# First experts of a two-block kernel: two fixed places instead of four, the plan four steps earlier, four places of 32 slots

## The chip, the cores and the metric

The kernel runs on one core of a Trainium2 chip, in one launch. The metric is the device time of that launch in microseconds (us). The kernel before took 2408.33 us as the median of three runs (2404.2 to 2413.0). One more execution was profiled; every row below comes from that one.

## What is computed

512 tokens of 1024 numbers go through two transformer blocks. Each block has a mixer (attention and a second branch) and a mixture of experts. The change concerns the experts of the first block alone:

```python
def hierarchical_moe(u, w_grp, b_grp, w_exp, b_exp, w_e_gate, w_e_up, w_e_down):
    ...                                    # every token picks 2 of 16 experts, with weights
    for e in range(N_EXPERTS):             # 16
        h = jax.nn.silu(t @ w_e_gate[e]) * (t @ w_e_up[e])     # 1024 -> 512
        y = y + comb[:, e:e + 1] * (h @ w_e_down[e])           # 512 -> 1024
```

Everything is float32. The three weights of an expert are 2 MB each, so the 16 experts read 96 MB. The 1024 assignments fall unevenly. Worked out from the reference's inputs, experts 0 to 15 get 27, 49, 13, 41, 17, 17, 29, 17, 96, 103, 87, 72, 131, 77, 77 and 171 tokens.

## The kernel before

**Stages.** First mixer, first experts (`moe1`), second mixer, second experts (`moe2`), one after the other on all engines. `moe1` and `moe2` share the function `experts`; its argument `nh` is 1 for `moe1` and 2 for `moe2`, and picks the tables at the top of the file.

**Places.** `experts` works through 16 places, in a fixed order. A place is a number of token slots and the weights of one expert. The first `FIXED` places hold experts 0, 1, ... by number, so that they can start before anybody knows how many tokens each expert has. The other places get the remaining experts by rank of their token count: `plan` (L839) computes the ranks on chip, and a table of constants says which rank goes to which place. Before, places 0 to 3 are fixed, with 128 slots each; places 6 and 11 are pairs (128 and 64 slots, `PAIRS`); of the rest, 5, 7, 9 and 12 have 96 slots, 8, 10, 13 and 15 have 64 (`SLOTS`), and 4 and 14 have 128. If an expert has more tokens than its place has slots, a loop at the end of `experts` makes one more pass for the rest.

**Work of a place.** `prep` builds a list of the place's tokens as a table of ones and zeros (`list_hot`, `oh`; on VectorE for the fixed places, on GpSimd for the others), TensorE multiplies it out (`prep2`, `pt<-paux,oh`), VectorE turns it into row numbers (`list_end`), GpSimd gathers the rows (`x_gather`, `xg`), and TensorE turns them (`x_turn`). Then come the products with gate and up (`gu`, into PSUM tiles `pm`), the activation, a turn of its result (`act_turn`), the product with down (`dn`, into `po`), and a scatter that adds the rows to `Y` in memory (`y_scatter`).

**Two kinds of product.** In places of 96 slots and more, each weight tile is split into a high part `whi` (ScalarE, L118) and a low part `wlo` (VectorE, L119), and each product is three matmuls, of 512 columns each: 48 for `gu` and 24 for `dn`. A pair adds 48 more for its second 64 slots. In places of 64 slots (`col`), the weight tile `wraw` is used as it is, in a slower float32 form that the trace records as two matmuls for each product, and gate and up stand side by side in two halves of the array (`col_gu`, `col_dn`): 32 records for `gu` and 16 for `dn`.

**Weights.** Gate and up of a place are two loads of 1 MB each, down is two more, so a place has six. The order of loads is that of use: `gu` of a place (4 loads), then `dn` of the place before it (2). They go to a ring of seven buffers. Four loads are issued before the stage, three by GpSimd at its start, and each further one by SyncE when the buffer seven loads back is free. A buffer is free when both its halves are split; in `col` places only when the matmuls have read it, for gate and up only when both have been read.

**Order.** The loop at the end of `experts` writes the instructions of each engine step by step, a step for each load; `at(step, f)` hangs other work on a step. `plan` is a generator whose parts hang on steps 0 to 6; the list of a place hangs `LEAD` steps (15, 12, 11, 10) ahead of its first product, its turns 5 and 2 steps ahead. `ctx_steps` hangs preparations of the second mixer on steps 6 to 88; `ctx_load` loads two last pieces for it.

## Time and profile before

| | us |
|---|---|
| median of three runs | 2408.33 |
| the profiled execution | 2409.98 |
| its span on the core | 2408.2 |
| in it, the last row of the router to the first product of an expert | 372 to 387 |
| products of the first experts | 387 to 716 |
| from there to the first load of the second mixer's rows | 716 to 727 |

The 1.8 us between the profiled execution's time and its span lie around the span. TensorE is busy 89% of the span, VectorE 57%, ScalarE 43%, GpSimd 28%. A busy TensorE is a matmul in flight; since matmuls overlap, the time from one start to the next tells its pace, not the length of one. In the first experts' stage the granted clock of TensorE is mostly the full 2.4 GHz.

### The profile page before, as it was taken

What the parts mean: (1) busy time and instruction counts of PE and PEld (TensorE: products, weight loads), DVE (VectorE), ACT (ScalarE), POOL (GpSimd) and SP (SyncE); (2) the same over time, 40 slices, a digit from 0 to 9 for tenths busy, and PEclk for the clock granted to TensorE, in tenths of its full rate; (3) what the DMA queues carried; (4) which work ended last, traced back from release to release, by engine and by line L of the source; (5) the groups of instructions that cost most, each with busy time, mean ns of one, the idle gap of its engine ahead of it and who ended that gap; (6) DMA issues with size and microseconds to landing.
All of it is one profiled execution on the core that took longest, in us unless ns stands there. A gap on an engine that the chain in (4) does not pass through costs nothing. (4 is left out here: it accounts for less than half of the span.)

```text
span 2408.2 us, 31803 instructions
## 1 busy us (share of the span) xinstructions
PE 2150.7 (89%) x11269; PEld 1395.7 (58%) x11269; DVE 1383.2 (57%) x2666; ACT 1037.6 (43%) x1577; POOL 681.6 (28%) x610
## 2 busy tenths in 40 slices
PE   6999986998988999999969899979999789988982
PEld 2655655775646886778857555635656445545520
DVE  5555697985647956653387555545555265527412
ACT  3333445874544444542236444324444244425301
POOL 2001235524323020000035343424344244333301
PEclk9999897999998999999979999989999989999996
DMA  8767447998977333323458999899999899999996
GB/s 275 246 204 263 170 158 263 376 338 304 360 270 215 86 96 122 90 65 115 140 193 302 345 401 393 305 378 401 397 393 368 301 403 377 386 395 401 382 415 231
DMA packets 208869, 681.65 MB, mean 283 GB/s; under 512 B 21261, under 2 KB 61029, under 8 KB 161601
## 3 DMA queue, kind: packets, MB, share of 16 engines
q1 hardware_dynamic: 185280, 607.88, 67.3%
q0 software_dynamic: 23136, 70.64, 10.7%
q8 instruction: 91, 1.49, 0.2%
q10 hardware_dynamic: 288, 1.05, 0.1%
q14 instruction: 74, 0.60, 0.1%
HBM read 642.69 MB, written 36.90 MB: 282 GB/s over the span
## 5 line engine op out<-in xcount | busy, mean ns | idle before, releaser
L119 DVE TENSOR_TENSOR wlo<-wraw,whi 128x1024 fp32r<-128x1024 f32 (+1 forms) x559 | 676.5, 1238 | 318.8 <-ACT whi L118 310.8
L118 ACT ACTIVATE whi<-wraw 128x1024 fp32r<-128x1024 f32 (+1 forms) x559 | 572.3, 1053 | 319.1 <-PE pm L81 120.8
L81 PE MATMUL pm<-whi,xh 128*128 128x512 f32 (+1 forms) x736 | 304.4, 414 | 3.5 <-ACT whi L118 3.5
L81 PE MATMUL pm<-wlo,xh 128*128 128x512 f32 (+1 forms) x736 | 297.5, 407 | 1.3 <-DVE wlo L119 1.2
L1196 POOL DMA_INDIRECT Y<-eo,isc x52 | 102.4, 1969 | 593.2 <-ACT eo L1195 251.5
L81 PE MATMUL pm<-whi,xl 128*128 128x512 f32 (+1 forms) x640 | 260.8, 407 | 0.0
L81 PE MATMUL pm<-wraw,xh 128*64 128x512 f32 (+1 forms) x1280 | 245.1, 614 | 14.9 <-DMA wraw<-in_w_gu 14.9
L81 PEld LDWEIGHTS pm<-whi,xh 128*128 128x128 f32 (+1 forms) x736 | 136.4, 185 | 47.3 <-ACT whi L118 4.2
L927 POOL TENSOR_SCALAR oh<-slots,plan 128x64 bf16<-128x64 f32 (+3 forms) x168 | 157.4, 1045 | 0.3
L81 PEld LDWEIGHTS pm<-wlo,xh 128*128 128x128 f32 (+1 forms) x736 | 130.3, 177 | 42.7 <-DVE wlo L119 2.6
L993 POOL DMA_INDIRECT xg<-U,ig x52 | 93.2, 1792 | 199.1 <-issue 112.6
L81 PEld LDWEIGHTS pm<-wraw,xh 128*64 128x64 f32 (+1 forms) x1280 | 65.8, 128 | 141.0 <-issue 108.3
L81 PEld LDWEIGHTS pm<-whi,xl 128*128 128x128 f32 (+1 forms) x640 | 116.7, 182 | 38.6 <-issue 0.9
L81 PE MATMUL po<-wraw,ah 128*64 128x512 f32 (+1 forms) x640 | 126.1, 606 | 14.0 <-DMA wraw<-in_w_dn 13.6
L81 PE MATMUL po<-whi,ah 128*128 128x512 f32 (+1 forms) x320 | 128.3, 401 | 0.0
L81 PE MATMUL po<-whi,al 128*128 128x512 f32 (+1 forms) x320 | 125.8, 393 | 0.9 <-DVE al L1160 0.9
L81 PE MATMUL po<-wlo,ah 128*128 128x512 f32 (+1 forms) x320 | 125.7, 393 | 0.0
L1005 PEld LDWEIGHTS pt<-ident,xg 64*128 64x128 f32 (+3 forms) x416 | 57.3, 197 | 80.2 <-DMA xg<-U,ig 34.4
L1005 PE MATMUL pt<-ident,xg 64*128 64x64 f32 (+3 forms) x416 | 69.6, 291 | 38.2 <-DMA xg<-U,ig 36.6
L1016 DVE TENSOR_TENSOR xl<-pt,xh 128x512 fp32r<-128x512 f32 (+1 forms) x52 | 32.5, 625 | 122.2 <-ACT xh L1014 122.0
L1014 ACT ACTIVATE xh<-pt 128x512 fp32r<-128x512 f32 (+2 forms) x60 | 31.3, 522 | 147.0 <-PE pt L1005 138.0
L81 PEld LDWEIGHTS po<-wraw,ah 128*64 128x64 f32 (+1 forms) x640 | 35.7, 127 | 90.9 <-issue 60.7
(618 smaller groups left out, 3994.8 us busy)
## 6 DMA issues: line engine op xcount, KB each, us to landing
wraw<-in_w_gu SPq DMA_DIRECT2D x254, 1024.0 KB
wraw<-in_w_dn SPq DMA_DIRECT2D x127, 1024.0 KB
wraw<-in_w_e_down SPq DMA_DIRECT2D x32, 1024.0 KB
wraw<-in_w_e_up SPq DMA_DIRECT2D x31, 1024.0 KB
wraw<-in_w_e_gate SPq DMA_DIRECT2D x30, 1024.0 KB
wraw<-in_w_in SPq DMA_DIRECT2D x58, 512.0 KB
mz<-in_w_ada SPq DMA_DIRECT2D x80, 256.0 KB
wraw<-in_w_mod SPq DMA_DIRECT2D x26, 512.0 KB
```

The costliest lines, as they stand in the source:

```text
L81: self.nc.tensor.matmul(out, lhsT, rhs, start=start, stop=stop)
L118: nc.scalar.activation(h, v, AF.Copy)
L119: nc.vector.tensor_sub(l, v, h.bitcast(F32))
L927: (eng or self.nc.gpsimd).tensor_scalar(oh[:, c, :], self.slots[:, 0:n], poscol(c), None, op0=OP.is_equal)
L993: self.nc.gpsimd.indirect_dma_start(out=B.xg[0:B.n, :], out_offset=None, in_=self.U, in_offset=bass.IndirectOffsetOnAxis(ap=B.ig[:, :1], a ...
L1005: self.nc.tensor.transpose(B.xt[:, k * n:k * n + n], B.xg[0:n, 4 * h2 + k:1024:8], self.ident[0:n, 0:n])
L1014: nc.scalar.activation(B.xh[:, d, 0:n], pv, AF.Copy)
L1016: nc.vector.tensor_sub(lo, pv, B.xh[:, d, 0:n].bitcast(F32))
L1196: nc.gpsimd.indirect_dma_start(out=self.Y[:, :], out_offset=bass.IndirectOffsetOnAxis(ap=B.isc[:, :1], axis=0), in_=o, in_offset=None, com ...
```

## The change

Six tables change, all for `nh` = 1. Two places are fixed instead of four. The pairs are places 4 and 10. Places 6, 8, 12, 14 and 15 have 96 slots, 5 and 9 have 64, 2, 3, 7 and 11 have 32; 0, 1 and 13 have 128. In all there are 1504 slots, before 1792. With the token counts above, each of the experts has a place that holds it, before and after; the tightest is the fourth of the movable ones, 96 tokens in 96 slots. The six parts of `plan` hang on steps -4, -3, -1, 0, 1 and 2, and lists of places that need the plan not before step 3.

In a place of 32 slots `col_gu` has four products side by side: gate and up of two slices of the inner dimension at a time, whose halves `col_act` (new) adds up. `dn` of `col` places is now done by `row_dn`, which also takes four at a time there, and the scatter adds the halves.

```diff
-FIXED = {2: 2, 1: 4}
-PAIRS = {2: (7, 16), 1: (6, 11)}
+FIXED = {2: 2, 1: 2}
+PAIRS = {2: (7, 16), 1: (4, 10)}
...
+PLAN = {2: (0, 1, 2, 3, 4, 5), 1: (-4, -3, -1, 0, 1, 2)}
...
-         1: ((5, 7, 9, 12), (8, 10, 13, 15))}
+         1: ((6, 8, 12, 14, 15), (5, 9), (2, 3, 7, 11))}
...
+        for a in range(2):
             for s, v in enumerate((gv, uv)):
-                self.mm(B.pg[hf, s], B.xf[:, j, 0:64], v[:, k, :], j == 0, j == 7)
+                k = 2 * q + a
+                p = n * (s + 2 * a if B.col == 4 else s)
+                j = 4 * kk + k
+                self.mm(B.pg[p:p + n], B.xf[:, j, 0:n], v[:, k, :], j == (a if B.col == 4 else 0),
+                        j == (6 + a if B.col == 4 else 7))
+
+    def col_act(self, B, stage):
+        nc, ea, n = self.nc, self.ea, B.n
+        if stage == 0:
+            a = B.a = ea.tile([128, 512], F32, name="ea")
+            if B.col == 4:
+                b = B.b = ea.tile([128, 512], F32, name="eb")[0:64]
+                nc.scalar.activation(b, B.pg[0:64], AF.Copy)
+                nc.vector.tensor_add(b, b, B.pg[64:128])
+                nc.scalar.activation(a[32:64], b[0:32], AF.Silu)
+            else:
+                nc.scalar.activation(a[0:64], B.pg[0:64], AF.Silu)
+        elif B.col == 4:
+            nc.vector.tensor_mul(B.b[0:32], B.b[32:64], B.a[32:64])
+            B.b = B.b[0:32]
...
-        for i in range(7):
+        for i in PLAN[nh]:
             at(i, next, plan, None)
...
+                for i, f in enumerate(((prep, b, B), (prep2, B), (prep3, B), (self.x_gather, B))):
+                    at(max(s0 - lead[i] - o, PLAN[nh][-1] + 1 + i if b >= fixed else -99), *f)
                 for h2 in range(2):
-                    at(s0 - lead[4 + h2] - o, self.x_turn, B, h2)
-                    at(s0 - lead[4 + h2] - o + 0.5, self.x_split, B, h2)
+                    i = max(s0 - lead[4 + h2] - o, PLAN[nh][-1] + 5 + h2 if b >= fixed else -99)
+                    at(i, self.x_turn, B, h2)
+                    at(i + 0.5, self.x_split, B, h2)
...
-                                self.col_dn(B, hf, s, raws[i], q, hf == nh - 1)
+                            elif what == "dn" and q == 0:
+                                self.row_dn(B, 0, s, raws[i], True)
```

Where this moves instructions most is the start of the stage. On GpSimd, before, the plan stands around the gather of place 2, and the first list that needs it (128 slots, `oh<-slots,plan`) comes after the gather of place 3:

```order
L853 TENSOR_SCALAR plank<-slots 128x4
L854 TENSOR_TENSOR plano<-plank,ident 16x16
L993 DMA xg<-U_111,ig 128x1024
L857 TENSOR_SCALAR plano<-plank,planc 16x16
...
L882 TENSOR_SCALAR bpos<-plan 128x4 x2
L1499 DMA rows_3832<-in_ctx 128x1024
L993 DMA xg<-U_111,ig 128x1024
L270 DMA gsc<-mod_108 128x8
L927 TENSOR_SCALAR oh<-slots,plan 128x128 x4
```

On GpSimd at the same point after the change:

```order
L855 TENSOR_SCALAR plank<-slots 128x2
L856 TENSOR_TENSOR plano<-plank,ident 16x16
L859 TENSOR_SCALAR plano<-plank,planc 16x16
...
L884 TENSOR_SCALAR bpos<-plan 128x4 x2
L929 TENSOR_SCALAR oh<-slots,plan 128x32 x8
L929 TENSOR_SCALAR oh<-slots,bpos 128x64 x4
L1515 DMA rows_3836<-in_ctx 128x1024
L995 DMA xg<-U_111,ig 32x1024 x2
```

The gathers of places 2 and 3 now stand behind the whole plan and behind twelve list operations, eight of them for these two places.

On TensorE before, where place 0 starts (`pt<-ident,xg` are turns of gathered rows, `pm<-whi,xh` is the first product):

```order
L1005 MATMUL pt<-ident,xg 128x128 x8
...
L1005 MATMUL pt<-ident,xg 128x128 x4
L81 MATMUL pm<-whi,xh 128x512
L81 MATMUL pm<-wlo,xh 128x512
```

On TensorE at the same point after the change:

```order
L1007 MATMUL pt<-ident,xg 128x128 x8
L867 MATMUL pt<-ident,pos 16x128 x4
L1007 MATMUL pt<-ident,xg 128x128 x4
L83 MATMUL pt<-planm,plant 128x16 x5
L83 MATMUL pm<-whi,xh 128x512
L83 MATMUL pm<-wlo,xh 128x512
```

The plan's first nine matmuls stood among the products of place 0 and now stand ahead of the first of them.

## Rows read from the trace of the kernel before

**Rows 1.** Windows: start:end, length, busy by engine (count), clock, DMA share, GB/s

```profile
372.00:387.00 15.00, 4.47 (x25) 3.40 (x25) 8.25 (x42) 2.90 (x5) 5.81 (x10) 0.50 0.63 221
387.00:520.00 133.00, 128.44 (x606) 100.74 (x607) 116.97 (x182) 104.71 (x132) 71.96 (x72) 0.97 1.01 371
520.00:600.00 80.00, 71.69 (x341) 46.47 (x341) 48.19 (x85) 43.27 (x68) 30.79 (x25) 0.99 0.86 289
600.00:716.00 116.00, 113.66 (x516) 68.84 (x516) 65.19 (x83) 59.33 (x80) 30.99 (x23) 0.99 0.90 329
716.00:727.00 11.00, 0.00 (x0) 0.00 (x0) 0.76 (x2) 0.68 (x1) 1.40 (x1) 0.60 0.42 67
```

**Rows 2.** Timeline of SyncE: start, length, issue of a load

```profile
655.50 0.34 SPq L105 DMA_DIRECT2D wraw<-in_w_e_gate  x1
668.95 0.33 SPq L105 DMA_DIRECT2D wraw<-in_w_e_up  x1
```

**Rows 3.** Timeline of TensorE: split products, then a place of 64 slots

```profile
655.24 0.39 PE L81 MATMUL po<-wlo,ah 128*128 128x512 f32 x1
...
664.09 0.39 PE L81 MATMUL pm<-whi,ah 128*128 128x512 f32 x1
...
665.27 3.65 PE L81 MATMUL pm<-wraw,xh 128*64 128x512 f32 x16
...
669.50 3.65 PE L81 MATMUL pm<-wraw,xh 128*64 128x512 f32 x16
```

**Rows 4.** DMA queues from 387 to 706: packets, MB, share of 16 engines

```profile
DMA packets 18152, 109.74 MB, mean 344 GB/s; under 512 B 2387, under 2 KB 2899, under 8 KB 6739
...
q1 hardware_dynamic: 13215, 92.95, 75.3%
q0 software_dynamic: 4917, 16.53, 19.7%
```

**Rows 5.** Groups by shape in 1200 to 2000, TensorE (second experts): busy, mean ns

```profile
L81 PE MATMUL pm<-wraw,xh 128*32 128x512 f32 x320 | 42.2, 643 | 0.0
...
L81 PE MATMUL po<-wraw,ah 128*32 128x512 f32 x160 | 23.1, 596 | 3.4 <-DMA wraw<-in_w_dn 3.3
```

**Rows 6.** Groups in 387 to 716, VectorE and ScalarE: busy, mean ns, idle before

```profile
L119 DVE TENSOR_TENSOR wlo<-wraw,whi 128x1024 fp32r<-128x1024 f32 x144 | 173.0, 1226 | 35.8 <-ACT whi L118 34.2
...
L118 ACT ACTIVATE whi<-wraw 128x1024 fp32r<-128x1024 f32 x143 | 148.0, 1056 | 34.6 <-PE pm L81 20.0 <-PE po L81 5.9 <-SPq L1432 4.6
```

**Rows 7.** Timeline, start of the stage: plan, lists, first products

```profile
379.64 0.35 POOL L851 TENSOR_SCALAR plank<-cnt 128x16 f32<-128x16 f32 x1
...
396.03 3.68 POOL L862 COPY plant<-pcol 16x128 f32<-16x128 f32 x1
...
413.69 5.32 POOL L927 TENSOR_SCALAR oh<-slots,plan 128x128 bf16<-128x128 f32 x4
...
386.88 0.80 PE L81 MATMUL pm<-whi,xh 128*128 128x512 f32 x1 [1.63 <-ACT whi L118]
...
398.48 1.06 PE L81 MATMUL pt<-planm,plant 16*128 16x16 f32 x8
...
418.36 0.48 PE L81 MATMUL po<-whi,ah 128*128 128x512 f32 x1
```

**Rows 8.** Windows of ten microseconds (columns as in rows 1)

```profile
480.00:490.00 10.00, 7.14 (x30) 4.80 (x29) 7.87 (x9) 9.54 (x19) 0.00 (x0) 0.83 1.02 428
690.00:700.00 10.00, 10.00 (x48) 4.44 (x48) 1.44 (x2) 1.55 (x3) 1.40 (x1) 1.00 1.03 384
```

**Rows 9.** Timeline of TensorE: two waits that are not for weights

```profile
484.54 0.71 PE L1555 MATMUL pt<-ident,rows 128*128 128x128 f32 x4 [1.91 <-DVE xh L1016]
...
598.82 1.09 PE L1005 MATMUL pt<-ident,xg 128*128 128x128 f32 x4 [4.14 <-DMA xg<-U,ig]
```

**Rows 10.** Timeline at the stage's end: last products, first load after

```profile
712.32 3.65 PE L81 MATMUL po<-wraw,ah 128*64 128x512 f32 x16
...
726.64 0.34 SPq L1746 DMA_DIRECT2D yx<-Y  x1
```

More of the change, by code (lines that the diff above doesn't have):

```diff
@@ L1030, in mm_gu, with col_gu @@
                 B.bias("gu", B.pg[hf, s][0:64], s, hf, False)
-    def col_gu(self, B, hf, kk, gv, uv, q):
+    def col_gu(self, B, kk, gv, uv, q):
+        n = B.n
         if kk == 0 and q == 0:
-            p = self.pm.tile([128, 512], F32, name="pm")
-            for s in range(2):
-                B.pg[hf, s] = p[64 * s:64 * s + 64]
-        for k in range(2 * q, 2 * q + 2):
-            j = 4 * kk + k
-            for s, v in enumerate((gv, uv)):
-                self.mm(B.pg[hf, s], B.xf[:, j, 0:64], v[:, k, :], j == 0, j == 7)
-    def col_dn(self, B, hf, jj, v, q, last):
-        j = 2 * jj + q
-        if hf == 0 and j == 0:
-            p = self.px.tile([128, 512], F32, name="po", tag="px")
-            B.po = [p[0:64], p[64:128]]
-        for s in range(2):
-            self.mm(B.po[s], B.ah[hf][:, j, :], v[:, q, 512 * s:512 * s + 512],
-                    j == 0 and hf == 0, j == 3 and last)
+            B.pg = self.pm.tile([128, 512], F32, name="pm")
+        for a in range(2):
+            for s, v in enumerate((gv, uv)):
+                k = 2 * q + a
[17 more added lines that the diff above has]
+            B.b = B.b[0:32]
+        else:
+            B.b = B.a[0:64]
+            nc.vector.tensor_mul(B.b, B.pg[64:128], B.b)
     def row_gu(self, B, k, v):
@@ L1070, in row_gu, with row_dn @@
                 self.mm(B.pg[s][n * hf:n * hf + n], B.xf[:, k, 0:n], v[:, 0, c0:c0 + 512], False, k == 7)
-    def row_dn(self, B, hf, jj, v):
+    def row_dn(self, B, hf, jj, v, last):
         n = B.n
@@ L1078, in row_dn @@
             for s in range(2):
-                B.bias("dn", B.po[s], s, 0, True)
+                if B.bias:
+                    B.bias("dn", B.po[s], s, 0, True)
         for q in range(2):
@@ L1083, in row_dn @@
                 self.mm(B.po[i], B.ah[hf][:, 2 * jj + q, :], v[:, q, 512 * s:512 * s + 512],
-                        hf == 0 and jj == 0 and i > 1, hf == 1 and jj == 1 and (q == 1 or B.col == 4))
+                        hf == 0 and jj == 0 and (i > 1 or not B.bias and (q == 0 or B.col == 4)),
+                        last and jj == 1 and (q == 1 or B.col == 4))
     def row_act(self, B, stage):
@@ L1110, in act @@
     def act(self, B, hf, stage):
+        if B.col:
+            return self.col_act(B, stage)
         nc, ea = self.nc, self.ea
@@ L1147, in act_split @@
             B.ah[hf] = ah.bitcast(F32)
-            nc.scalar.activation(B.ah[hf], B.at.rearrange("p (k q) -> p k q", k=4), AF.Copy,
-                                 scale=1.0)
+            nc.scalar.activation(B.ah[hf], B.at.rearrange("p (k q) -> p k q", k=4), AF.Copy)
             return
@@ L1320, in experts @@
                 o = 2 * nh if B.second else 0
-                at(s0 - lead[0] - o, prep, b, B)
-                at(s0 - lead[1] - o, prep2, B)
-                at(s0 - lead[2] - o, prep3, B)
-                at(s0 - lead[3] - o, self.x_gather, B)
+                for i, f in enumerate(((prep, b, B), (prep2, B), (prep3, B), (self.x_gather, B))):
+                    at(max(s0 - lead[i] - o, PLAN[nh][-1] + 1 + i if b >= fixed else -99), *f)
                 for h2 in range(2):
-                    at(s0 - lead[4 + h2] - o, self.x_turn, B, h2)
-                    at(s0 - lead[4 + h2] - o + 0.5, self.x_split, B, h2)
+                    i = max(s0 - lead[4 + h2] - o, PLAN[nh][-1] + 5 + h2 if b >= fixed else -99)
+                    at(i, self.x_turn, B, h2)
+                    at(i + 0.5, self.x_split, B, h2)
             if rows[b]:
@@ L1407, in experts @@
                             elif q == 0:
-                                self.row_dn(B, hf, s, raws.pop(i))
+                                self.row_dn(B, hf, s, raws.pop(i), hf == 1)
                             else:
@@ L1413, in experts @@
                             if what == "gu" and s == 1:
-                                self.col_gu(B, hf, kk, raws[i - 1], raws[i], q)
-                            elif what == "dn":
-                                self.col_dn(B, hf, s, raws[i], q, hf == nh - 1)
+                                self.col_gu(B, kk, raws[i - 1], raws[i], q)
+                            elif what == "dn" and q == 0:
+                                self.row_dn(B, 0, s, raws[i], True)
                             if q == 1 and (what == "dn" or s == 1):
```

## Prediction

> **What bounds the kernel now.** The change touches one stage, so I first cut that stage out of the span with windows [rows 1]. Read in each line the busy time of TensorE (the first number after the length) against the length, then the share of the DMA engines (last but one). From 387 to 716 TensorE has a matmul in flight in 314 of 329 us. The DMA engines are busy 1.01 of the time up to 520, and 0.86 and 0.90 after it. So two resources are nearly full, and the question is which waits for which.
>
> SyncE's timeline tells [rows 2]: a load of weights goes out at 655.50, the next at 668.95. In between no buffer of the ring is free, since TensorE reaches the place whose buffers come next only at 665.27, and gives two back at 668.92 [rows 3]. TensorE itself runs at full pace there: 39 matmuls from 655.24 to 664.09 start every 0.233 us. So after 520 the transfers wait for TensorE. Up to 520 both are full. TensorE is the bound of the stage, and the DMA engines stand just behind it: their load from 387 to 706 is 75.3% for weights and 19.7% for the software queue, 95% of 319 us [rows 4].
>
> **The change part by part.** *Products.* A full place (96 or 128 slots) is 72 matmuls of 0.233 us, 16.8 us. A place of 64 is 48 records; 16 take 3.65 [rows 3], so 11.0 us. A place of 32 isn't in this stage, but the second experts have such products: 320 records in 42.2 us of busy time for gate and up, 160 in 23.1 for down [rows 5], 0.13 and 0.14 us each. 48 records are then 6.5 us. Bounds: half the place of 64 (5.5 us, if four products cost what two do) and the whole of it (11.0, if they don't overlap); I take 6.5, the same shape in this trace. Places go from 10 full, 2 pairs and 4 of 64 to 8 full, 2 pairs, 2 of 64 and 4 of 32: minus 33.6, minus 22.0, plus 26.0, so 29.6 us less on TensorE. The number of turns stays. Alone this would put TensorE's end at 686 instead of 716.
>
> *Transfers.* The weights stay. A load of 1.05 MB costs 0.753 x 319 / 88.6 loads = 2.71 us of all engines [rows 4]. Of the software queue's 62.8 us, some 6.8 are five loads of 0.5 MB for the second mixer; the other 56 us are gathers and scatters of 1568 slots, 0.036 us for a slot. 1792 - 1504 = 288 slots less give back 10.3 us. So the DMA engines need 294 us for what they did in 304, and can't end much before 387 + 294 = 681. That is close to TensorE's 686. With places that leave TensorE little to do, I expect the engines to change roles: the DMA becomes the bound, and its time runs from the moment when it last has to wait for a buffer.
>
> *Splits.* Two full places less are 24 of 144 tiles less for VectorE (1.23 us each) and ScalarE (1.06) [rows 6], 29 and 25 us. Neither bounds the stage, since both wait for others; I count nothing. Without that cover it would be a gain.
>
> *The head.* This decides the DMA's start. Loads 4 to 16 (13 of them) need no product of place 2; at 2.71 us each and some 5 us of gathers they are through at about 379 + 40 = 419. Loads 17 and 18 need the buffers of place 2's first gate and up, which TensorE gives back after place 0's down product and the first 8 products of place 2. Before, the down product starts at 418.36 [rows 7] and ends 24 x 0.233 plus a turn later, at 424.4. Three things shift this. The plan's nine matmuls (1.6 us with their wait, from 398.48) and four transposes leave the products, minus 2.2. In exchange they stand before the first product, behind GpSimd's plan, which starts at 379.64 and had one copy of 3.68 us; the first product comes at 386.88 before, and I put it 3 us later (bounds 0 and 6: the copy hidden by the gathers' landing, or the copy and the two reductions that VectorE now does in between laid end to end). And the lists of places 2 and 3, eight operations and four for the pair, stand on GpSimd ahead of both gathers; four took 5.32 us, so twelve take 16. TensorE, with lists and turns in its order, waits for them; queued behind are VectorE's list end and ScalarE's copies, and with these the splits. From about 397, when the plan can be ready, 16 us of lists and a gather put place 2's rows near 418, where TensorE would ask for them near 412. I take 6 us of waits; bounds 0 (smaller lists are quicker) and 15. With 2.1 us for the first eight products (16 records of 0.13), the buffers come at 424.4 + 3 - 2.2 + 6 + 2.1 = 433; bounds 424 and 445.
>
> SyncE reads the expert's number for places 2 and 3, too. The plan has it before the first product, and load 10 isn't due before about 397; I cost it at nothing.
>
> *From there.* 79 loads x 2.71 = 214 us, gathers and scatters of 1296 slots x 0.036 = 47, the second mixer's pieces 6: 267 us of work. At the share of 1.02 that the engines show when never idle [rows 8] this is 262 us. As a cross-check: 82.8 MB of weights, 11.5 of slots (16.5 less 2.6 for 1568, so 8.9 KB each) and 2.6 are 97 MB, in 262 us 370 GB/s; the stretch to 520 moved 371 [rows 1]. The last load lands at 433 + 262 = 695. What may still make the DMA idle is a pair, 28 us of products against 16 of loads; but before either pair TensorE starves, and seven buffers hold 19 us of loads, so nothing.
>
> *Waits that go.* TensorE's wait of 1.91 us for a split ahead of a preparation of the second mixer, and 4.14 for a gather [rows 9], are on TensorE's path now. They would lie beside the DMA then. They are worth nothing more.
>
> *The end.* After the last landing come the last split (3.5 us for two halves) and six products, 4.9 us: 700, against 716 before (712.32 + 3.65 [rows 10]). From there to the second mixer's first load, at 726.64, the way stays: two scatters one behind the other; the last has 96 rows instead of 64, the one before 96 instead of 128. I leave it at 10.7 us. The rest of the span is the same program; in the second experts one list moves a step, beside products. A last piece that SyncE loaded in mid-stage now follows the last weights; it isn't needed before 727.
>
> Sum: 716 - 700 = 16 us less. The profiled execution took 2409.98, so 2394; the median lies 1.65 below it, so 2392.
>
> A rule speaks against this: the Trainium skill (DMA: Bandwidth & Descriptors, "Where 436 GB/s comes from") says that from HBM the memory side binds, at some 358 GB/s. The trace shows more, 428 and 384 GB/s over ten microseconds [rows 8]. By the skill's figure the 97 MB would take 271 us, an estimate, and the sum would be 2401; by the rows it is 2392, and I stay with the rows.
>
> **The rivals.** *The transfers stay slower.* From 520 to 600 the engines moved 289 GB/s at a share of 0.86, so 336 in busy time, where the two other stretches give 367 and 366 [rows 1]. If the mix of gathers and pairs there is what the whole stage gets, 97 MB at 336 x 1.02 = 343 GB/s take 283 us: 2413, no change. For it: scatters keep coming. Against: there are fewer slots, and [rows 8] shows more.
>
> *The clock eats it.* From 480 to 490 TensorE idled for 2.9 us, and the granted clock was 0.83 on average, so in part the lower level, 1.2 GHz [rows 8]. Six cheap places and more waits would bring this after each of them: first products at half pace. With some 9 products at twice 0.233 it is 2 us each time, 12 in all, on the path only where TensorE is behind: 2404 if all of it is. The Trainium skill (TensorE: Matmul & The Clock Gate, "HAM oscillation") warns of idle gaps between bursts of matmuls; the clock of that window agrees.
>
> *The head is late: slower.* Each microsecond by which place 2's rows come later than I say ends the stage a microsecond later, since the DMA stands still meanwhile. From 449 on instead of 433 the gain is gone; at 460, if the twelve lists take twice their time beside the splits and the second gather waits for the first, it is 2419.
>
> *It doesn't fit.* If the chip counts 97 tokens where I count 96, the loop makes one more pass: six loads with nothing beside them, 16 us, the products, 17, lists, gather and scatter, some 15: 2440.
>
> **How the numbers follow.** Forecast 0.60, slower transfers 0.08, clock 0.10, late head 0.12, no fit 0.03, more gain than my bounds 0.07. The forecast's own range: buffers at 424 and a share of 1.03 end at 2380; buffers at 445, at 2404. For the range I take 2378, TensorE's floor of 686, to 2408, which takes in the clock and leaves out most of the other three. About 0.3% (7 us) can be told from no change. Faster: the forecast, the larger gain, and half of the clock, 0.72. Slower: two thirds of the late head, and no fit, 0.11. Within: slower transfers, the rest of the clock and of the late head, 0.17.
>
> **What would show it.** Right: from place 3 on the DMA share stays near 1.02 without dips, TensorE waits for weights (`wraw`, `whi`) in the places of 32 and 64, and the last product ends near 700. The head: place 2's first record near 431, with waits on lists or rows ahead of it. Wrong: gaps of 10 us between loads after 450, as in [rows 2]; a clock below 0.9 in the middle of the stage with TensorE never waiting; or a pass after the last place.

## The result: slower by 0.6%, and the profile after

The changed kernel takes 2424.29 us (median of 4), the kernel before 2409.01 beside it: a ratio of 1.0064, 95% interval 1.0042 to 1.0087. The forecast was 2392, within 2378 to 2408. The profiled execution took 2422.89 us, span 2421.1.

All of it is lost in the stage that was changed: from the first load of the next stage's rows to the end of the span, the changed kernel's trace is 2.8 us shorter than that of the kernel before (1678.8 against 1681.6). These are the windows of the changed kernel, in the columns of [rows 1]:

```profile
372.00:387.00 15.00, 8.45 (x36) 6.18 (x36) 7.02 (x27) 5.07 (x7) 5.61 (x12) 0.50 0.71 258
387.00:520.00 133.00, 113.36 (x543) 74.86 (x543) 73.84 (x125) 67.83 (x100) 58.04 (x73) 0.90 0.86 316
520.00:600.00 80.00, 62.96 (x289) 34.12 (x288) 42.26 (x96) 35.69 (x59) 27.78 (x30) 0.85 0.87 305
600.00:716.00 116.00, 102.59 (x496) 72.05 (x495) 77.76 (x101) 69.19 (x90) 32.16 (x23) 0.94 0.94 351
716.00:727.00 11.00, 10.69 (x50) 7.50 (x50) 10.06 (x11) 8.39 (x10) 0.00 (x0) 1.00 0.33 50
```

Against [rows 1], TensorE's first number is lower in each stretch from 387 to 716, and so is the DMA share up to 520, 0.86 in place of 1.01. The last product ends at 734.2 instead of 716.0. From the first gate and up product to the last down product, in one window for each kernel, first before and then after:

```profile
386.88:715.97 329.09, 313.91 (x1460) 216.16 (x1460) 230.47 (x349) 207.44 (x278) 133.74 (x120) 0.98 0.93 337
```

```profile
385.85:734.22 348.37, 297.88 (x1403) 193.59 (x1402) 206.30 (x332) 183.73 (x258) 119.40 (x126) 0.91 0.86 312
```

TensorE is busy 16.0 us less, as a change that takes products away should have it. But it idles 348.37 - 297.88 = 50.5 us where it idled 15.2. And the granted clock falls from 0.98 to 0.91.

Along the stage the two engines take turns. Windows of the changed kernel, cut where the DMA share changes:

```profile
410.00:430.00 20.00, 19.64 (x107) 14.70 (x105) 12.79 (x34) 11.45 (x16) 13.24 (x14) 1.00 0.58 201
430.00:480.00 50.00, 36.46 (x180) 21.97 (x179) 23.78 (x45) 19.87 (x32) 17.54 (x30) 0.84 1.02 380
480.00:510.00 30.00, 27.56 (x132) 15.89 (x131) 14.47 (x23) 16.36 (x28) 10.48 (x6) 0.92 0.68 234
510.00:570.00 60.00, 47.43 (x217) 28.07 (x216) 36.17 (x85) 30.09 (x47) 19.43 (x21) 0.86 1.00 362
570.00:600.00 30.00, 25.53 (x120) 13.26 (x119) 12.86 (x21) 11.93 (x18) 10.42 (x11) 0.89 0.67 227
600.00:672.40 72.40, 58.99 (x302) 38.85 (x300) 41.18 (x59) 34.61 (x48) 26.68 (x19) 0.93 0.97 359
672.40:707.00 34.60, 34.60 (x156) 26.47 (x157) 28.85 (x35) 26.56 (x32) 3.92 (x3) 0.95 0.91 339
707.00:734.20 27.20, 26.81 (x119) 18.58 (x117) 19.02 (x19) 17.89 (x22) 2.98 (x2) 1.00 0.50 145
```

From 430 to 480, 510 to 570 and 600 to 672 the DMA engines are all but full, and there TensorE idles 13.5, 12.6 and 13.4 us, most of its 50.5. In between, the DMA share falls to 0.68 and 0.67. From 672 on TensorE is full, and the DMA runs out of loads.

What TensorE waits for is told by sums of waits, 385 to 735 (waiting line, what it waits for: us in total, times, longest):

```profile
PE pt L83 <- POOL oh L929: 18.2, 17, 6.9
PE pt L1007 <- DMA xg<-U,ig: 10.3, 2, 6.0
PE pt L1158 <- ACT xh L1014: 4.2, 1, 4.2
```

A list from GpSimd (1.8 us in the kernel before), gathered rows (4.1 before), and ScalarE's copies ahead of a turn. The weights are seldom late. ScalarE's splits wait for a landed load:

```profile
ACT whi L120 <- DMA wraw<-in_w_e_gate: 7.3, 2, 5.7
ACT whi L120 <- DMA wraw<-in_w_e_up: 2.6, 1, 2.6
```

In all that is 9.9 us (1.1 in the kernel before), and the longest of them, ahead of the first pair, costs TensorE 2.6 us. The waits of SyncE for a buffer of the ring can't decide it: they add up to 268 us here and to 257 in the kernel before, since the ring is nearly always taken.

The longest wait, 13 us, lies behind the second pair, place 10. Timelines of GpSimd, ScalarE, VectorE and TensorE there (start, length, engine, line, operation, in brackets the idle time before it and who ended it):

```profile
648.94 2.17 POOL L1212 DMA_INDIRECT Y<-eo,isc  x1 [9.82 <-ACT eo L1211]
...
663.35 2.36 POOL L1212 DMA_INDIRECT Y<-eo,isc  x1 [10.80 <-DVE eo L1209]
665.28 6.95 POOL L929 TENSOR_SCALAR oh<-slots,plan 128x96 bf16<-128x96 f32 x4
...
660.94 1.26 ACT L1208 ACTIVATE eo<-pm,slw 64x512 f32<-64x512 f32 x2 [9.10 <-DMA Y<-eo,isc]
...
661.65 1.42 DVE L1209 SCALAR_TENSOR_TENSOR eo<-pm,slw,eo 64x512 f32<-64x512 f32 x2 [9.32 <-ACT eo L1208]
...
657.58 1.92 PE L83 MATMUL po<-wraw,ah 128*32 128x512 f32 x16
666.36 0.24 PE L83 MATMUL pt<-paux,oh 128*96 128x6 bf16 x1 [6.86 <-POOL oh L929]
...
671.79 0.24 PE L83 MATMUL pt<-paux,oh 128*96 128x6 bf16 x1 [2.68 <-POOL oh L929]
...
672.38 0.77 PE L83 MATMUL pm<-whi,xh 128*128 128x512 f32 x1
```

A pair scatters twice (the second half of its slots is `L1208`, `L1209`). There is one output buffer (`eo`), so ScalarE's copy for the other half waits until the first scatter has landed (648.94 to 660.94, 12 us), VectorE behind it, and GpSimd with the second scatter at 663.35. Behind that scatter on GpSimd stands the list of place 15, and for that list TensorE waits, with place 13's products queued behind it. Place 11, which lies in between, takes 32 slots, and its down product is over in 1.92 us.

The 12 us lie beside full DMA engines (a share of 1.03 from 648.9 to 661.0). The scatter of place 14, 96 rows, when no load was left, let go of the buffer 5.5 us after its issue:

```profile
729.39 1.42 POOL L1212 DMA_INDIRECT Y<-eo,isc  x1 [13.53 <-ACT eo L1211]
...
734.93 0.68 ACT L1211 ACTIVATE eo<-po,slw 96x512 f32<-96x512 f32 x1 [5.82 <-DMA Y<-eo,isc]
```

So a full DMA seems to be part of why such waits are long. No run here takes the loads away to show how much.

### The profile page after: what moved, and what is told of

It reads as the page before. It is cut to its first block, busy times and chain, and to the rows that moved or that the text cites. A ratio compares the mean times of both kernels' runs of the same rounds, so it can differ in the third digit from the quotient of the medians.

```text
span 2421.1 us, 31654 instructions
## 1 busy us (share of the span) xinstructions
PE 2139.4 (88%) x11221; PEld 1375.2 (57%) x11221; DVE 1359.4 (56%) x2640; ACT 1015.5 (42%) x1559; POOL 647.3 (27%) x618
## 5 line engine op out<-in xcount | busy, mean ns | idle before, releaser
L121 DVE TENSOR_TENSOR wlo<-wraw,whi 128x1024 fp32r<-128x1024 f32 (+1 forms) x535 | 650.0, 1244 | 340.6 <-ACT whi L120 332.0
L120 ACT ACTIVATE whi<-wraw 128x1024 fp32r<-128x1024 f32 (+1 forms) x535 | 545.8, 1052 | 344.7 <-PE pm L83 113.1
L83 PE MATMUL pm<-wraw,xh 128*64 128x512 f32 (+1 forms) x1344 | 254.0, 635 | 13.4 <-DMA wraw<-in_w_gu 13.4
L83 PE MATMUL pm<-whi,xl 128*96 128x512 f32 (+1 forms) x608 | 247.5, 407 | 0.0
L929 POOL TENSOR_SCALAR oh<-slots,plan 128x32 bf16<-128x32 f32 (+3 forms) x176 | 153.1, 1019 | 0.3
L83 PEld LDWEIGHTS pm<-whi,xl 128*96 128x96 f32 (+1 forms) x608 | 110.5, 182 | 37.1 <-issue 0.9
L83 PE MATMUL po<-whi,ah 128*96 128x512 f32 (+1 forms) x304 | 123.5, 406 | 2.3 <-ACT ah L1172 2.2
L83 PE MATMUL po<-whi,al 128*96 128x512 f32 (+1 forms) x304 | 121.4, 399 | 0.6 <-DVE al L1174 0.6
L83 PE MATMUL po<-wlo,ah 128*96 128x512 f32 (+1 forms) x304 | 121.5, 400 | 0.0
L1018 DVE TENSOR_TENSOR xl<-pt,xh 128x384 fp32r<-128x384 f32 (+1 forms) x48 | 29.4, 612 | 122.0 <-ACT xh L1016 121.9
L1016 ACT ACTIVATE xh<-pt 128x384 fp32r<-128x384 f32 (+2 forms) x56 | 28.7, 513 | 143.2 <-PE pt L1007 134.7
```

Of the source, the lines that this page charges most:

```text
L83: self.nc.tensor.matmul(out, lhsT, rhs, start=start, stop=stop)
L120: nc.scalar.activation(h, v, AF.Copy)
L121: nc.vector.tensor_sub(l, v, h.bitcast(F32))
L929: (eng or self.nc.gpsimd).tensor_scalar(oh[:, c, :], self.slots[:, 0:n], poscol(c), None, op0=OP.is_equal)
L1016: nc.scalar.activation(B.xh[:, d, 0:n], pv, AF.Copy)
L1018: nc.vector.tensor_sub(lo, pv, B.xh[:, d, 0:n].bitcast(F32))
```

## The theory and its rivals

**Queue and latency.** Each gathered place needs one round through the engines' queues: list on GpSimd, sum on TensorE, list end on VectorE, gather, turn. The round stands at fixed steps of the order, behind scatters that wait for TensorE's results. A cheap place shortens the steps, but not the round, so TensorE waits; and after the wait its products run at the lower clock. The expectations call this theory Pairs where it is about the waits behind the pairs, Queue, Lists or Buffer where it is about one link of the round. The rivals: **Head:** the loss comes from the two first gathered places. **Order:** it comes from what stands behind the pairs and last. **Rows:** from the two buffers of gathered rows. **Halves:** from the extra adds of four products side by side.

All runs but c1 and c2 have the code of the changed kernel, so its new `dn` of places of 64 as well; what differs are its tables (`FIXED`, `PAIRS`, `SLOTS` and the new `PLAN`, four and not six) and the lines shown.

This table has all the kernels: ratio to the kernel before, run beside them on the same chip, with its 95% interval; then from the trace the length of the stage, from the first gate and up product to the end of the last product, TensorE's busy time in it, and the rest. Whole executions of one kernel scatter by some 10 us. The stage's start moves too, between 384.6 and 390.5, mostly with the first mixer, which is the same in all; so I compare lengths and not ends. Two traces of one kernel differ in length by up to 1.9 us (329.1 and 331.0 for the kernel before). I read steps from the length, and verdicts from the ratio.

| kernel | ratio, interval | length | busy | idle |
|---|---|---|---|---|
| before | | 329.1 | 313.9 | 15.2 |
| before again (c1) | 1.0009, 0.9992 to 1.0027 | 331.0 | 317.6 | 13.4 |
| changed | 1.0064, 1.0042 to 1.0087 | 348.4 | 297.9 | 50.5 |
| f1 plan alone | 0.9975, 0.9955 to 0.9994 | 327.3 | 313.3 | 14.0 |
| f4 + two fixed places | 1.0016, 0.9999 to 1.0033 | 334.9 | 310.6 | 24.3 |
| e6 + new order, six of 64 | 0.9997, 0.9980 to 1.0014 | 337.7 | 310.4 | 27.3 |
| e2 places of 32, old order | 0.9991, 0.9976 to 1.0006 | 327.9 | 304.3 | 23.6 |
| e1 changed, four fixed | 1.0021, 1.0001 to 1.0040 | 343.4 | 311.2 | 32.2 |
| e3 changed, two `eo` | 0.9999, 0.9984 to 1.0013 | 336.9 | 297.0 | 39.8 |
| e5 changed, early lists | 1.0029, 1.0016 to 1.0043 | 344.2 | 297.7 | 46.5 |
| e4 changed, other order | 0.9998, 0.9984 to 1.0012 | 332.6 | 295.3 | 37.4 |
| f3 changed, three `xg` | 1.0027, 1.0003 to 1.0051 | 347.9 | 300.5 | 47.4 |
| g1 changed, halves apart | 1.0068, 1.0044 to 1.0093 | 345.8 | 299.9 | 45.9 |
| e7 three cures | 0.9983, 0.9966 to 1.0000 | 334.1 | 296.3 | 37.9 |
| e8 cures, four fixed | 0.9964, 0.9948 to 0.9981 | 330.7 | 309.9 | 20.8 |
| c3 e8 again | 0.9964, 0.9946 to 0.9981 | 329.5 | 307.9 | 21.6 |
| c4 e8 with places of 64 | 0.9987, 0.9968 to 1.0006 | 332.4 | 312.6 | 19.8 |
| g2 e8, halves apart | 0.9985, 0.9965 to 1.0005 | 327.6 | 306.1 | 21.5 |
| c2 before, two cures | 0.9982, 0.9961 to 1.0002 | 331.0 | 316.3 | 14.7 |
| g3 before, plan, two cures | 0.9970, 0.9948 to 0.9991 | 326.8 | 313.1 | 13.7 |

## Experiments: the parts of the change

**f1, the plan alone.** Fixed places, pairs and kinds of the kernel before, with the plan's new steps:

```
-        for i in range(7):
+        for i in PLAN[nh]:                # (-4, -3, -1, 0, 1, 2)
             at(i, next, plan, None)
```

> The kernel before with one part of the change alone: the plan four steps earlier; four fixed places, kinds, order and products as before. The forecast's step (the plan ahead of the first products costs 3 us there and takes 2.2 us out of the products): the first gate and up product within 3 us of the kernel before, no other difference, 2406 to 2412. Rival: GpSimd's plan in the head is what makes the rows of place 2 and 3 late, then the stage is 5 us or more longer here too, 2413 or more.

0.9975, 2401.4 us, and a stage 2 to 4 us shorter than in the two traces of the kernel before. From the first gather to the first product it is 12.1 us, before 11.4 and 11.3, so the plan ahead of it costs 0.8 us at most. A small gain, where I had costed it at a small loss; whether the plan or the new `dn` brings it, no run separates.

**f4, two fixed places in place of four, besides.** In the old order; places 2 and 3 are gathered, of 64 slots:

```
-FIXED 1: 4   SLOTS 1: ((5, 7, 9, 12), (8, 10, 13, 15))
+FIXED 1: 2   SLOTS 1: ((5, 7, 9, 12), (2, 3, 8, 10, 13, 15))
```

> The kernel before with two parts of the change: two fixed places and the plan earlier; places 2 and 3 become gathered places of 64 slots, all else as before (no place of 32, the pairs at 6 and 11, the old order). TensorE gets 11.6 us less than before. Theory HEAD: the first gathered places cost more than that, 2412 to 2420. Theory ORDER (the loss comes from the kinds that stand behind the pairs and last): 2398 to 2409.

1.0016, 2413.2 us, with an interval above that of f1, and a stage 7.6 us longer than f1's, though TensorE is busy 2.7 us less: Head. Its timeline of SyncE shows the step as forecast: the loads stand still until place 2 gives buffers back, about 433.

```profile
421.99 0.34 SPq L107 DMA_DIRECT2D wraw<-in_w_e_gate  x1
433.77 0.34 SPq L107 DMA_DIRECT2D wraw<-in_w_e_up  x1
```

TensorE pays for it when it has caught up with the loads. The second of its waits is for VectorE, which stands behind a split whose load landed late (ScalarE waited 13.2 us for it, to 462.98):

```profile
458.44 1.94 PE L83 MATMUL po<-wraw,ah 128*64 128x512 f32 x8 [1.68 <-DMA wraw<-in_w_e_down]
467.09 0.25 PE L83 MATMUL pt<-paux,oh 128*128 128x6 bf16 x4 [6.71 <-DVE xl L1018]
```

**e6, the changed kernel without a place of 32.** One line differs:

```
-1: ((6, 8, 12, 14, 15), (5, 9), (2, 3, 7, 11))}
+1: ((6, 8, 12, 14, 15), (2, 3, 5, 7, 9, 11))}
```

> The changed kernel with all its cheap places of 64 slots (places 2, 3, 7 and 11 too), so without the four products side by side; order and plan as in the changed kernel. It gives TensorE 3.65 - 1.92 us more for each 16 records, 20.8 us in all, and the DMA 128 slots, 4.6 us. If TensorE's products set the pace: 2440 to 2445. If the cheap place's gain only turned into waits for lists and rows, the longer products fill those waits: 2418 to 2430.

0.9997, 2410.2 us: some 15 us faster than the changed kernel, below my range of either theory, though TensorE and the DMA have more to do. The stage is 10.7 us shorter, and 2.8 longer than that of f4, which has another order of nearly the same kinds. So order and pairs alone cost 2.8 us, and the four places of 32 cost 10.7 instead of giving 20.8. Of the 20.8 us only 310.4 - 297.9 = 12.5 show in TensorE's busy time (the granted clock over the stage is 0.91, in e6 0.94), and the idle time grows by 23.2.

Where that happens is seen in the first pair, place 4. Windows of five microseconds, columns as before; the changed kernel first, then e6:

```profile
460.00:465.00 5.00, 5.00 (x16) 3.69 (x17) 2.81 (x4) 1.54 (x2) 0.00 (x0) 0.66 1.01 370
465.00:470.00 5.00, 5.00 (x24) 3.65 (x23) 3.19 (x4) 4.34 (x5) 0.00 (x0) 1.00 1.04 431
470.00:475.00 5.00, 1.47 (x7) 0.75 (x5) 4.22 (x5) 2.23 (x4) 0.00 (x0) 0.95 1.01 426
475.00:480.00 5.00, 4.37 (x13) 3.43 (x14) 4.00 (x18) 2.51 (x8) 3.87 (x6) 0.50 1.01 415
```

```profile
460.00:465.00 5.00, 5.00 (x29) 1.87 (x26) 2.96 (x3) 2.49 (x3) 3.73 (x7) 1.00 1.04 322
465.00:470.00 5.00, 5.00 (x24) 3.61 (x23) 2.93 (x3) 4.06 (x5) 0.00 (x0) 1.00 1.01 407
470.00:475.00 5.00, 5.00 (x24) 3.72 (x23) 4.89 (x9) 4.58 (x9) 0.31 (x1) 1.00 1.01 426
475.00:480.00 5.00, 5.00 (x24) 3.83 (x23) 3.54 (x14) 1.55 (x4) 3.93 (x6) 1.00 1.01 399
```

The changed kernel begins the pair's products 6.3 us ahead of e6 (458.56 against 464.91; its stage had begun 1.0 us earlier), having waited for a split whose load came late; they run at a clock of 0.66, so in part at 1.2 GHz, then TensorE waits 4.2 us for ScalarE, and the next run at 0.50, all at 1.2 GHz. It ends them 2.8 us behind (488.1 against 485.35). The cheap place's lead is used up within one pair.

**e2, places of 32 alone, in the old order:**

```
-1: ((5, 7, 9, 12), (8, 10, 13, 15))}
+1: ((5, 7, 9, 12), (8,), (10, 13, 15))}
```

> The kernel before (2409) in its own order, with its four fixed places and its late plan; of the change only the products of a place of 32: three of its four places of 64 take 32 slots and four products side by side. Theory: the cheap product is a gain where the order around it stays (13.5 us of TensorE and 3.5 of the DMA less): 2395 to 2404. Rival: a place that costs TensorE little only brings it sooner to the next list or rows, and the loss is the cheap place's own: 2409 or more.

0.9991, by the ratio between the two: TensorE is busy 9.6 us less than before and idles 8.4 us more. The cheap product costs little in itself; almost all that it saves turns into waits.

**e1, the changed kernel with four fixed places:**

```
-FIXED 1: 2   SLOTS third row (2, 3, 7, 11)
+FIXED 1: 4   SLOTS third row (7, 11)
```

> The changed kernel (2424) with four fixed places in place of two; from place 4 on the kinds and their order are those of the changed kernel. It leaves the head's lists out and gives TensorE 20.6 us and the DMA 7 us more work. Theory HEAD (the loss comes from the first gathered places, whose lists and rows are late, so that SyncE's loads stand still from 419.12 to 429.64 and from 434.50 to 450.19, 26 us): those gaps go, and the stage ends about 26 - 7 us earlier, near 2405. Theory PAIRS (the loss comes after each pair, where one output buffer makes the second scatter, and the lists behind it on GpSimd, late; TensorE idles 13 us from 659.5 to 672.5): the waits after the pairs stay, and the time stays between 2420 and 2440.

1.0021, 2412.4 us: faster than the changed kernel, with 13 us more on TensorE. Head is in it, but the wait behind pair 10 stays (TensorE idles from 657.9 to 669.5, but for the list's sums), and of the 19.3 us that the stage had grown by, 5.0 go. Head's price of 26 us was too high: in the second of its two gaps, from 434.5 to 450.2, only the issues of loads paused, while the DMA engines were full with seven loads under way (a share of 1.02).

## Experiments: the wait behind a pair

**e3, two output buffers** (`al` and `eb` go from two buffers to one for the room):

```
-        self.nraw, self.nsplit, self.neo = (7, 9)[nh - 1], 6, nh
+        self.nraw, self.nsplit, self.neo = (7, 9)[nh - 1], 6, 2
...
```

> The changed kernel with two output buffers in this stage in place of one (two scratch tiles go from two buffers to one for the room). Theory PAIRS: the waits of ScalarE for a scatter (16.1 and 14.3 us in all) go, the lists behind the pairs come in time, and of TensorE's 13 us at 659.5 and 6 at 532 to 543 most goes: 2405 to 2414. Theory HEAD or a bound by TensorE in the last four full places: 2420 to 2425.

0.9999, 2408.9 us, as Pairs forecast, and the stage 11.5 us shorter. ScalarE no longer waits for a scatter. But the second scatter still does, now for the first one itself, and the list behind it:

```profile
643.74 2.10 POOL L1212 DMA_INDIRECT Y<-eo,isc  x1 [9.85 <-ACT eo L1211]
...
656.34 1.69 POOL L1212 DMA_INDIRECT Y<-eo,isc  x1 [9.07 <-DMA Y<-eo,isc]
657.59 3.84 POOL L929 TENSOR_SCALAR oh<-slots,plan 128x96 bf16<-128x96 f32 x4
```

Both add to `Y`, and the program orders them for that. The Trainium skill (DMA: Bandwidth & Descriptors, "Rules for kernel authors") asks for a wait between accumulating transfers on the same bytes. These two have no row in common: by the code the halves of a pair hold different tokens of one expert, and a slot without a token adds to a spare row of its own, 512 plus its number, of which a full first half uses none. So this wait is for the tensor as a whole. No run here tried without.

**e5, each list four steps earlier,** ahead of the scatters; three list buffers:

```
-LEAD 1: (15, 12, 11, 10, 5, 2)
+LEAD 1: (19, 12, 11, 10, 5, 2)
...
```

> The changed kernel (2424), in which only GpSimd's order differs: each list is made four steps earlier (19 in place of 15 ahead of its place, with three list buffers in place of two), so that the list of place 15 stands ahead of the two scatters of pair 10 instead of behind them, and that of place 9 ahead of pair 4's. TensorE's order is unchanged. Theory QUEUE (TensorE idles from 659.5 to 672.5 because its list stands on GpSimd behind a scatter that waits): those 13 us and some 2 at 532 go, 2408 to 2412. Rival BUFFER (the single output buffer stops ScalarE and VectorE for 9 us each with all splits behind them, so TensorE waits for splits at the same place instead): 2419 to 2425.

1.0029, 2417.4 us, between Queue and Buffer; the stage is 4.1 us shorter. TensorE's row in the same place:

```profile
654.34 1.93 PE L83 MATMUL po<-wraw,ah 128*32 128x512 f32 x16
659.57 0.49 PE L83 MATMUL pm<-whi,xh 128*128 128x512 f32 x1 [3.03 <-ACT whi L120]
...
672.24 0.91 PE L1158 MATMUL pt<-ident,ea 96*128 96x96 f32 x4 [3.79 <-DVE slsb L943]
```

The wait for the list is gone. In its place stand a wait for the split that ScalarE, stopped by the output buffer, makes late, and one for VectorE. Both causes hold, one behind the other.

**e4, a full place behind each pair:**

```
-1: ((6, 8, 12, 14, 15), (5, 9), (2, 3, 7, 11))}
+1: ((7, 9, 11, 13, 15), (8, 14), (2, 3, 6, 12))}
```

> The changed kernel with the same kinds of places, the same head and the same pairs, but another order from place 5 on: a full place behind each pair, single cheap places in between, a place of 64 as the last but one. Theory PAIRS (a cheap place behind a pair leaves GpSimd no time for the scatters and the next list): TensorE's 13 us idle behind the second pair and 6 behind the first go, 2404 to 2412. Theory HEAD: what is lost by 450 stays lost, 2420 to 2426.

0.9998, 2407.6 us, as Pairs forecast, and the stage 15.7 us shorter, with not one product more or less. The list of place 15 starts at 655.36 there, and TensorE, with 17 us of place 11 to do, waits 2.9 us for its four parts. With places of 64 the order mattered little (f4 and e6, 2.8 us); with places of 32 it does.

## Experiments: rows and halves

**f3, three buffers of gathered rows** (`al` and `eb` again with one):

```
-name="xg")
+name="xg", bufs=3)
...
```

> The changed kernel with three buffers for gathered rows in place of two (two scratch tiles go to one buffer for the room), so that a gather needn't wait until TensorE has turned the rows of two places earlier (GpSimd's waits for that add up to 28.9 us). Theory ROWS: TensorE's waits for rows, 6.0 us at 445 and 4.3 at 584, go and with them 8 to 10 us: 2412 to 2416. Theory LISTS (the gather is late because its list is): the waits stay, 2420 to 2426.

1.0027, 2418.4 us, in neither range; its interval overlaps that of the changed kernel, so a gain of some us isn't excluded. In the trace, of an execution that took 2425.9, the stage shows none: 347.9 against 348.4, so there Rows falls. GpSimd's 28.9 us of waits for row buffers shrink to about 1, and TensorE's 4.3 us at 584 go. But two waits for lists come at 598 and 600, 2.9 us, place 11's down product ends at 659.44 against 659.50, and the last product at 734.41 against 734.22. What the scratch tiles with one buffer less cost isn't separated. The 6 us at 445 stay; the gather's row and TensorE's:

```profile
431.76 1.58 POOL L996 DMA_INDIRECT xg<-U,ig  x1 [0.30 <-issue]
...
446.32 1.09 PE L1008 MATMUL pt<-ident,xg 128*128 128x128 f32 x4 [5.79 <-DMA xg<-U,ig]
```

From issue to use are 14.6 us for one gather of 128 rows, beside loads that keep the DMA engines busy.

**g1, copies of both halves first, then the adds:**

```
+        for s in range(2) if B.col == 4 else ():
+            nc.scalar.activation(o[:, s * 512:s * 512 + 512], B.po[s], AF.Copy, scale=B.w)
         for s in range(2):
             d = o[:, s * 512:s * 512 + 512]
             if B.col == 4:
-                nc.scalar.activation(d, B.po[s], AF.Copy, scale=B.w)
                 nc.vector.scalar_tensor_tensor(d, B.po[2 + s], B.w, d, op0=OP.mult, op1=OP.add)
```

> The changed kernel, in which the scatter of a place of 32 writes both halves on ScalarE first and then adds on VectorE twice, in place of copy, add, copy, add. Theory HALVES: ScalarE's second copy waits for VectorE's first add behind VectorE's splits (2.77 us at 473.54), TensorE's wait of 4.16 us at 475.63 hangs on that, and so once in each place of 32: three to four times 2 to 4 us, 2410 to 2417 (the places of 32 of the second experts change too). Rival: the wait only passes to the next operation in the queue: 2420 to 2425.

Halves falls: 1.0068, 2427.2 us. The stage is 2.6 us shorter, little more than two traces of one kernel differ by. The wait at 475 is 3.34 us in place of 4.16; ScalarE's stall of 2.77 is gone, and what it waited for stands on VectorE behind the same splits.

## Experiments: the cures together

**e7** joins e3, e4 and e5. **e8** has four fixed places besides; **c3** is e8 again.

```
+LEAD 1: (19, ...), neo = 2, SLOTS 1: ((7, 9, 11, 13, 15), (8, 14), (2, 3, 6, 12))
+e8: FIXED 1: 4, third row (6, 12)
```

> The changed kernel with all three cures: the other order of kinds from place 5 on, two output buffers, and the lists four steps earlier. If they act on different waits: some 28 us less than the changed kernel, 2394 to 2400, faster than the kernel before. If they take away the same waits: 2404 to 2410.

> The same three cures with four fixed places in place of two, so that no list or rows stand in the way before place 4. TensorE gets 20.6 us and the DMA 7 us more work. Theory HEAD (the first gathered places cost 10 us or more): below the run with two fixed places by 3 to 8 us, 2390 to 2400. If TensorE is the bound again: 2405 to 2412.

> The four fixed places with the three cures once more, for a second trace and ten more times: 2396 to 2402, a ratio of 0.995 to 0.998, if the first measurement holds; 0.999 or more if it was scatter.

e7: 0.9983, 2405.5 us. Its stage isn't shorter than e4's: the cures take away the same waits. e8: 0.9964, 2398.2 us, and a stage 3.4 us shorter than e7's though TensorE is busy 13.6 us more, as Head forecast. c3: 0.9964 again, and both intervals end at 0.9981. This version beats both kernels, the one before by 0.36%, some 8.7 us.

What of it is due to the cheap places, three runs ask. **c4** gives e8 places of 64, **c2** puts the cures into the kernel before, **g3** cures and plan; **c1** is the kernel before again.

> The same as the run before it with its two places of 32 made places of 64, so without four products side by side. TensorE gets 3.65 - 1.92 us more for each 16 records, 10.4 us in all, and the DMA 2.3 us. If the cheap product pays once the waits are cured: 2404 to 2409. If TensorE waits there anyway: 2396 to 2401.

> The kernel before with the two cures alone, lists four steps earlier and two output buffers; places, kinds, order and products as in the kernel before. If the cures take waits that the kernel before has as well (4.14 us for rows, 12.9 us of ScalarE behind scatters): 2398 to 2403. If its full places already hide them: 2405 to 2410, and the gain of the four-place kernel with the cures comes from the cheap places.

> The kernel before with the plan four steps earlier and the two cures (lists earlier, two output buffers), but with its own order and no place of 32. If the plan (0.9975 alone) and the cures (0.9982 alone) make the gain of the four-place kernel with the cures, this one is as fast, 0.995 to 0.997, and the cheap places add nothing. If they need the cheap places: 0.998 to 1.000.

> The kernel before, unchanged, as a second trace of it: what two executions of one kernel differ by, stage by stage. Ratio 1.000, within 0.0015. If the four fixed places with the three cures win inside the first experts, this trace has its last product of the stage near 329 us after the first again, as the first trace had; if they win only by the scatter of the second experts between executions, that part (1487.9 us in the first trace) is 1475 to 1480 here.

c4: 0.9987, its stage 2.3 us longer than the mean of e8 and c3. So the cheap product is worth 2 to 6 us there, and the intervals overlap. c2 is at 0.9982 with a stage as long as before, g3 at 0.9970 with one as short as that of f1, the plan alone. The intervals of f1, g3, e8 and c3 overlap: the old kinds with the plan, with or without the cures, come as near as can be told. **g2**, e8 with g1's scatter, gives 0.9985, outside both its ranges and no gain:

> The four fixed places with the three cures (ratio 0.9964 twice) and the scatter of the run before. If the halves cost what they seem to, a further 2 to 4 us: 2394 to 2399, ratio 0.994 to 0.996. If not, 0.996 to 0.997.

Where e8 wins stays in part open. In its two traces the stage takes 330.7 and 329.5 us, before 329.1 and 331.0, so no less. From the stage's first product to that of the next stage it is 338.3 and 337.0 us, before 340.3 and 342.4; but from the first gather to that first product it takes 13.0 and 13.6 us, before 11.4 and 11.3. What is left of the 8.7 us there is some 2. The rest shows in the second experts: from their first gate and up product to their last product 1101.0 and 1106.5 us in e8 and c3, 1110.8 and 1114.2 in the kernel before, but 1101.7 in c2, which has the same code there as before. (The 1487.9 us that c1's expectation names for this part begin at a product of the second mixer, at 885.28.) No run tells a cause.

## Why the prediction was wrong, step by step

- **Products.** Right in size. Place 2's first 16 products of 32 slots took 1.92 us (at 427.68), 48 make 5.8; I took 6.5. The sum of 29.6 us showed as 16.0 of busy time. The granted clock, 0.91 over the stage in place of 0.98, took part of the rest. 16 products of a place of 64 take 3.65 us in [rows 3]; two such groups of the changed kernel, each behind a wait, took:

```profile
494.86 5.35 PE L83 MATMUL pm<-wraw,xh 128*64 128x512 f32 x16
...
585.83 5.98 PE L83 MATMUL pm<-wraw,xh 128*64 128x512 f32 x16
```

- **The head.** Right. I put the return of place 2's buffers at 433; load 17 went out at 429.64, after a pause in which the DMA share was 0.57. The plan cost 0.3 us (from the first gather to the first product 11.6, before 11.4) where I took 3, the waits for lists 3.3 in place of 6, since the twelve lists took 6.5 us and not 16:

```profile
419.12 0.35 SPq L107 DMA_DIRECT2D wraw<-in_w_e_gate  x1
429.64 0.34 SPq L107 DMA_DIRECT2D wraw<-in_w_e_up  x1
```

- **From there: the step that failed.** I let the DMA run on without idle time from 433, 262 us to a last landing at 695, put what a pair may make it idle at "nothing", since before either pair TensorE would starve, and let TensorE end 4.9 us behind the last landing. The first 50 us went so, at a share of 1.02. But in the same 50 us TensorE idled 13.5, for rows, a split and a copy, and then held the ring: from 480 to 510 the share was 0.68. Place 4 did begin with a short wait for a load, but place 10 didn't: the ring was full, held by a TensorE that had waited for lists and rows. From 433 to the last load's issue it was this:

```profile
433.00:707.00 274.00, 227.57 (x1075) 143.16 (x1074) 154.30 (x263) 136.74 (x200) 88.03 (x88) 0.89 0.91 335
```

  A share of 0.91 in place of 1.02 is some 30 us of idle time in 274, and behind that issue TensorE had 27 us still to do. Over the whole stage 0.86 x 348 = 300 us are work, near my 294, and 48 idle.
- **Waits that go.** I took only the kernel before's waits [rows 9], and called them hidden. I didn't ask what new ones appear when TensorE reaches each list and each gather sooner. They are the 35 us by which its idle time grew: 16 of them for lists, 6 for rows, the rest for splits and copies. This is the same error seen from TensorE: I replaced one bound by another, as if the two engines shared nothing but the ring, where in the trace they take turns.
- **Splits** bound nothing by their load, as said; but they stand in the queues in which a scatter's wait stops them (e5).
- **The end.** The four full places at the end keep TensorE full to the last (10.69 of 11 us from 716 on), with a DMA share of 0.33: here TensorE is the bound, and the 4.9 us had no DMA to follow. From the last product to the first load of the next stage 8.1 us (734.2 to 742.35), I left 10.7.
- **The rivals.** *Slower transfers* falls up to 520: 316 GB/s at a share of 0.86 are 367 in busy time, the old rate. *It doesn't fit* falls, no pass comes after. *Late head* didn't happen in its own terms; f4 shows that even a head in time costs 7.6 us of what f1 has. *Clock* was a true mechanism, priced as 12 us if TensorE is behind all the time; the 13.6 us of the products that didn't show are of that size, but no run separates them. Of the signs that I named as wrong, gaps of 10 us after 450 came (the issues at 580.17 and 591.84, for one), and the clock below 0.9 came (0.84 from 430 to 480), though not with a TensorE that never waits.
- **The sum.** 734.2 instead of 700 for the last product, 34 us. By the chain of runs, in lengths of the stage from f1's 327.3: two fixed places 7.6, order and pairs 2.8, places of 32 10.7, together the 348.4; and the gain of 16 that I expected came from none of them.

## What to carry over

A cheaper step on the bounding engine gains only as far as everything that step needs can come sooner. So before a product is made cheaper, list for each step what it takes from other queues, and how long that round lasts from its last free input; where the step becomes shorter than the round, the difference is a wait. And a bound isn't handed from one engine to another by comparing their sums: the trace must show the second one waiting for nothing but work. To tell such steps apart, measure a stage from its own first product: what lies ahead moved its start by up to 6 us here.

## What the runs showed that I had not expected

- GpSimd's list of four operations on 128x96 takes 2.05 us at 453.14, when VectorE does nothing, and 6.95 at 665.28, when VectorE splits (busy 6.22 of 7.1 us). Windows around the two, columns as above:

```profile
453.00:455.20 2.20, 2.20 (x24) 0.94 (x20) 0.00 (x0) 0.00 (x0) 2.18 (x6) 1.00 1.04 330
...
665.20:672.30 7.10, 0.74 (x4) 0.48 (x4) 6.22 (x7) 3.63 (x5) 7.03 (x5) 0.50 1.02 382
```

  The Trainium skill (GPSIMD Engine Reference, "1. Specifications") names contention with VectorE instructions that have two inputs in SBUF, as the low halves of a split have. The rows agree, by a factor of three; no run here changes VectorE's work alone.
- A scatter of 128 rows kept its buffer for 12 us (648.94 to 660.94), though by my estimate from the share of the DMA engines its slots cost 0.036 us each.
- A kernel with more work on its bounding engine was faster: e6 against the changed kernel, 12.5 us more of busy time and 10.7 less of stage.
